# Attention values for 512 queries at once, and one MLP product moved ahead of the sums of its input

## The chip, the cores and the metric

The kernel runs on one core of a Trainium2 chip. The metric is the device time of one execution in microseconds. Engines, as the profile names them: PE is TensorE (matrix products and transposes), PEld its weight loads, DVE is VectorE, ACT is ScalarE, POOL is GpSimd, SP is SyncE, which issues DMAs.

## The reference

One layer of a hybrid block on 512 tokens of width 1024, in fp32, and a last norm:

```python
n = rmsnorm(h, g_mix)
gq, gk, gv, gr, z_gf, z_gb, cq, ckv, kr, z_ma, z_mb = split(n @ w_in)
y_gla = gla_branch(gq, gk, gv, gr, z_gf, z_gb, ...)     # 4 heads of gated linear attention
y_mla = mla_branch(cq, ckv, kr, positions, ...)         # 8 heads of softmax attention
h = h + (sigmoid(z_ma) * y_gla + sigmoid(z_mb) * y_mla) @ w_out
m = rmsnorm(h, g_mlp)
h = h + square(relu(m @ w_ff1)) @ w_ff2                 # 1024 -> 4096 -> 1024
return rmsnorm(h, g_final)

# in mla_branch, for each of 8 heads (128 value columns each):
s = einsum('bhqd,bhkd->bhqk', q, k)
p = softmax(s, axis=-1)
o = einsum('bhqk,bhkv->bhqv', p, v)
```

The change touches the last line of `mla_branch` and the order of work at the start of `m @ w_ff1`.

## The kernel before

**Precision.** A product in fp32 is done as three products of numbers split in a high and a low part (`mm3`: high by high, high by low, low by high). A split is one ACT instruction for the high part and one on DVE for the low part. Each `mm3` is thus three TensorE instructions, each with a weight load of its own.

**Order.** The body does not issue instructions at once. It records them, and `flush` gives them to a list scheduler (`Due`) with a cost for each instruction; it sets the order on each engine under the recorded dependencies, and may reorder the products on TensorE. All instructions are issued by one helper, so all of them carry line 232 in the profile, and groups are told apart by the names of tiles. PSUM has eight banks of 128x512, four with the tag `mm` and four with the tag `at`.

**Attention.** One loop over n runs over the 32 pairs of head and query tile (8 heads, 4 tiles of 128 queries). Round n normalises the pair of tiles before (in even rounds), computes scores and exponents of tile n (`s`, `top`, `e`), flips tile n - `LAG_B` (3 rounds later), and multiplies values at c = n - `LAG_C` (6 rounds later). `att_normalise` takes two tiles: one reciprocal of both sums on DVE, the first tile scaled on ACT, the second on DVE. `att_flip(head, qt)` transposes the four key tiles of one query tile into one `at` bank `tp` and splits that into `pT`, high and low, kept for a pair of query tiles (4 key tiles by 256 queries). `att_values(head, half)` multiplies one pair of query tiles: four key tiles, each one `mm3` of 128x256, so 12 TensorE instructions a half and 24 a head, into one half of the bank `av`. Halves are issued at odd c. Behind the second half `merge` multiplies by the gate on DVE (`tb<-tb,av`) and adds the other branch on POOL. The last head merges each half by itself, since the output projection waits for it. In the same rounds the next pair of heads is projected (`uq`, `uk`, `uv`), and weights of the output projection (`bo10`, `bo11`) are split.

**Output projection.** `wo_product` forms seven products (Strassen-Winograd) of 512 columns in the banks `wox`, `wow` and `woz`.

**MLP.** m is transposed row by row (`ident,ms` into `mb` banks, gained by ACT and DVE). The up projection runs in eight `Quad`s of seven products (m = 1, 5, 2, 6, 3, 7, 4), each of 24 TensorE instructions of 128x256, planned at 2.88 us. Products 1, 2 and 3 read parts of m itself; products 5, 6, 7 and 4 read sums of such parts, which `combine` and `split_m` build on DVE and ACT once all rows of m are there (`four` in the trace: `four0` and `four1` for m = 5, `four2` and `four3` for 6, `four4` and `four5` for 7). Weights of a product are staged by DMA into `wf` tiles or sums `w0s`, `w1s`, and split into one of four pairs `hl0` to `hl3`. A quad holds three banks, x, z and w, taken from the ring `mms` (banks `mb0` to `mb3`) and given back after products 2, 3 and 4; `evacuate` reads a bank into a row tile (ACT for 1, 5 and 6; DVE for 2, 3 and 7). At the start quads 0 and 1 go side by side:

```python
    quads[1].multiply(2)
    split_m(7, r01, 2)
    fm.evacuate(1, range(4, KD))
    split_m(4, r10, 3)
    groups = [Group(qd) for qd in range(NQ)]
    for m in (5, 6):
        for q in range(2):
            quads[q].multiply(m)
```

The down projection (`Group`, banks `ab` from the ring `ats` among others) follows and is interleaved with the later quads.

Of the kernel before, what the change touches and what calls it, by code (L numbers as in the profile page):

```python
# [18 lines left out]
P = 128  # L19
# [373 lines left out]
def tile_block(ctx: ExitStack, tc: tile.TileContext, t, out: bass.AP):  # L393
# [28 lines left out]
    def u4(name, dt=F32R, shape=(P, 2, S)):  # L422
        return tl(list(shape), dt, "u4", 30, name)
# [113 lines left out]
    class Flipped:  # L537
# [8 lines left out]
        def rows(self, i, xs):  # L546
            half = i // 2
            if half not in self.banks:
                self.banks[half] = [ps("at", f"{self.name}b{half}{j}") for j in range(4)]
            for k in range(KD):  # L550
                at = (k // 4) * 256 + (i % 2) * P
                nc.tensor.transpose(
                    self.banks[half][k % 4][:, at : at + P], xs[:, k * P : (k + 1) * P], ident
                )
# [901 lines left out]
        nc.vector.tensor_scalar(b, b, tot[:, 1:2], None, op0=ALU.mult)  # L1456

    def att_flip(head, qt):
        e = probs.pop((head, qt))
        if qt % 2 == 0:  # L1460
            pTs[head, qt // 2] = [u4(f"pT{head}{qt}{x}", F32R, (P, NT, 256)) for x in range(2)]
        tp = ps("at", f"tp{head}{qt}")
        for k in range(NT):
            nc.tensor.transpose(tp[:, k * P : (k + 1) * P], e[:, k * P : (k + 1) * P], ident)
        hi, lo = pTs[head, qt // 2]
        c = slice((qt % 2) * P, (qt % 2 + 1) * P)
        split(hi[:, :, c], lo[:, :, c], tp.rearrange("p (k q) -> p k q", k=NT))

    def att_values(head, half):
        if half == 0:  # L1470
            avs[head] = ps("mm", f"av{head}")
        acc = avs[head]
        hi, lo = pTs.pop((head, half))
        _, _, vs, c = heads[head]
        for k in range(NT):
            vt = vs[k // 2]
            mm3(acc[:, half * 256 : (half + 1) * 256], vt[:, 0, k % 2, c], vt[:, 1, k % 2, c],
                hi[:, k, :], lo[:, k, :], k == 0, k == NT - 1)
        if head < MH - 1:
            if half == 1:  # L1480
                merge(head, acc, (0, 1))
        else:
            merge(head, acc, (half,))

    def merge(head, acc, halves_):

        p, c = head // 2, slice((head % 2) * HT, (head % 2 + 1) * HT)
        if p not in merged:
            merged[p] = u2(f"mx{p}"), u2(f"my{p}")
        y = g2[head]  # L1490
        tok = slice(halves_[0] * HT, (halves_[-1] + 1) * HT)
        nc.vector.scalar_tensor_tensor(y[:, tok], y[:, tok], 1.0, acc[:, tok], op0=ALU.add, op1=ALU.mult)
        for x in halves_:
            t_ = slice(x * HT, (x + 1) * HT)
            nc.gpsimd.tensor_tensor(merged[p][x][:, c], y[:, t_], y1[head][:, t_], op=ALU.add)
# [151 lines left out]
    rs = gla_squares(h, os)  # L1647
    gla_gated(h, os, rs)
    LAG_B, LAG_C = 3, 6
    units = up_units(1)  # L1650
    next(units)
    sums_of, flipping, span = {}, {}, {}
    for n in range(4 * MH + LAG_C - 1):
        if n % 2 == 0 and 2 <= n <= 4 * MH:
            att_normalise((n - 2) // 4, (n - 2) % 4)
        if n < 4 * MH:
            att_scores(n // 4, n % 4)
        if 2 <= n % 8 < 7:
# [12 lines left out]
        for x, at in (("y", (18, 26, 34)), ("z", (20, 28, 36))):  # L1671
            if n in at:
                p = at.index(n)
                to = (5, 6) if x == "y" else (7, 3)
                split_sum(wo_left[p], sums_of[p, x], *to, f"{x}o{p}", nc.gpsimd if p < 2 else nc.vector)
        if n in (19, 30):
            p = (19, 30).index(n)
            split_first(wo_left[p], merged[p][0], f"o{p}", nc.gpsimd)
        if n == 35:
            split_first(wo_left[2], merged[2][0], "o2")  # L1680
        if n in (11, 13):
            streamed(1, B11, (n - 11) // 2)
            split_streamed(1, (n - 11) // 2)
        if n in (21, 23):
            streamed(2, B21, (n - 21) // 2)
        if n == 15:
            load_w2(0, B11, w_out)
        if n == 17:
            load_w2(0, B21, w_out, B22)
        if n == 23:  # L1690
            load_onto(B21, B11, w_out)
        if n == 24:
            load_w2(0, B12, w_out)
            load_w2(0, B22, w_out)
        c = n - LAG_C
        if c >= 0 and c % 2 == 1:
            att_values(c // 4, (c % 4) // 2)
        if n == 33:
            load_onto(B21, B12, w_out)
        if c > 0 and c % 8 == 7 and c // 8 < NP - 1:  # L1700
            sums_of[c // 8, "y"], sums_of[c // 8, "z"] = merged_sums(c // 8, nc.gpsimd)
# [274 lines left out]
    class Quad:  # L1976
# [5 lines left out]
        def ready(self, m):  # L1982
            self.begun[m] = self.weights(m)

        def rows(self, i, j):
            return w1_block(self.q, i, j)

# [38 lines left out]
                wfs.back(item)  # L2026
            return ready

        def multiply(self, m):
            bank = {1: "x", 5: "z", 2: "w", 6: "x", 3: "z", 7: "x", 4: "x"}[m]  # L2030
            hl, wh, wl, keys = self.weights(m)
            begin = m in (1, 5, 2)
            if begin:
                self.banks[bank] = mms.take()
            bkey, acc = self.banks[bank]
            hi, lo = m_of[m]

            def run():
                for x in range(2):
                    c = slice(x * HT, (x + 1) * HT)  # L2040
                    f = slice(x * P, (x + 1) * P)
                    for k in range(KD // 2):
                        mm3(acc[:, c], wh[:, k, f], wl[:, k, f], hi[:, k, :], lo[:, k, :],
                            begin and x == 0 and k == 0, k == KD // 2 - 1, True)

            plan.add("PE", 2.88, run, keys + m_key[m], (bkey,))
            hls.back(hl)
            self.evacuate(m, bkey, acc)
            if m in (2, 3, 4):
                mms.back(self.banks[bank])  # L2050

        def evacuate(self, m, bkey, acc):
            if m in (5, 1, 6, 4):
# [278 lines left out]
    combine(r01, r11, r01, ALU.subtract)  # L2332
    combine(r10, msum, r10, ALU.subtract)
    quads[1].multiply(2)
    split_m(7, r01, 2)
    fm.evacuate(1, range(4, KD))
    split_m(4, r10, 3)
# [7 lines left out]
    for qd, g in enumerate(groups):  # L2345
        odd = quads[2 * qd + 1]
        g.multiply(1, 0)
        if qd:
            odd.multiply(7)
        g.multiply(1, 1, (2,))  # L2350
        odd.multiply(4)
        second = 5 if g.last else 2
        g.multiply(second, 0)
        g.multiply(1, 1, (3,))
        g.multiply(second, 1)
        if g.last:
            break
        even, odd = quads[2 * qd + 2], quads[2 * qd + 3]
        for m, between in ((5, 5), (3, None), (6, 1), (7, 2), (4, None)):
            for x in range(2):  # L2360
                g.multiply(m, x)
            if between:
                even.multiply(between)
        for m in (6, 3, 7):
            even.multiply(m)
        odd.multiply(5)
        even.multiply(4)
        for m in (1, 2, 6, 3):
            odd.multiply(m)
# [46 lines left out]
```

## Time and profile before

| what | number |
| --- | --- |
| runs | 737.72, 738.91 and 3364.55 us, median 738.91 |
| the profiled execution | 737.6 us |
| its span on the core | 735.9 us |
| PE busy | 726.7 us, 99% of the span, 4214 instructions |
| DVE busy | 606.2 us, 82% |
| ACT busy | 516.7 us, 70% |
| attention's values on TensorE | 307.6 to 375.2 us of the span |
| products with m = 5 begin | 425.09 us |

A row of the waits says which engine waited for which tile of which engine, and then the microseconds in total, how often, and the longest. A piece of the chain is a start, a length and the work. In rows of the timeline the brackets name the time that the engine was idle before and what released it. "x12" is the number of instructions put together; matmuls overlap, so that the length of one is more than the time from its start to that of the next.

### The profile page before, as it was taken

Reading aid. Unit: us, or ns where it says so; the run is one execution under the profiler, and the core shown is the slowest. Engines: PE = TensorE matmul, PEld = TensorE weight load, DVE = VectorE, ACT = ScalarE, POOL = GpSimd, SP = SyncE. Lnnn points to the kernel's source line nnn. Section 1 sums busy time; section 2 is a strip of 40 time slices with the busy share of each in tenths; the row PEclk is TensorE's granted clock in tenths of the full one; section 3 lists DMA queues with packets and bytes.
Section 4 is the critical chain, followed back from the end, with each engine's and each line's share of the span. In section 5 each row is a group of like instructions: output and inputs, shape, how many; then the busy total and the mean of one; then the engine's idle time right before and its main releaser. Section 6 shows DMA issues by size and latency. Waiting matters only on the chain.

```text
span 735.9 us, 11540 instructions
## 1 busy us (share of the span) xinstructions
PE 726.7 (99%) x4214; PEld 640.5 (87%) x4214; DVE 606.2 (82%) x959; ACT 516.7 (70%) x863; POOL 201.6 (27%) x208
## 2 busy tenths in 40 slices
PE   8999999999999999999999999999999999999996
PEld 7888888888898888899988999889988998889985
DVE  6694776759999769998988899878985798778885
ACT  7574666659999657989955798647864587448744
POOL 1133031301111215038753421321132212212433
PEclk9999999999999999999999999999999999999999
DMA  9969896652312223339996899998899997988993
GB/s 312 331 142 166 215 201 113 115 115 57 87 49 68 32 53 94 72 86 256 245 289 109 178 204 251 164 243 185 207 205 207 214 209 178 216 223 194 191 167 115
DMA packets 105050, 124.39 MB, mean 169 GB/s; under 512 B 16176, under 2 KB 68416, under 8 KB 104992
## 3 DMA queue, kind: packets, MB, share of 16 engines
q0 software_dynamic: 33024, 51.14, 41.9%
q1 hardware_dynamic: 71680, 71.97, 32.1%
q8 instruction: 33, 0.54, 0.3%
q10 hardware_dynamic: 288, 0.52, 0.2%
q14 instruction: 25, 0.20, 0.1%
HBM read 119.95 MB, written 2.10 MB: 166 GB/s over the span
## 4 chain that ended last, share of the span: by engine, by line
PE 93%; DVE 3%; ACT 2%; issue 1%; DMA 1%; POOL 1%; POOLq 0%; DVEq 0%; ACTq 0%
PE mb L232 25%; PE ab L232 16%; PE zb L232 4%; PE av L232 3%; PE s L232 3%; PE wox L232 3%; PE gvx L232 3%; PE zax L232 3%; PE grx L232 3%; PE first L232 3%; PE cq L232 2%; PE tp L232 2%; PE uv L232 2%; PE gvz L232 2%; PE ckv L232 1%; PE gq L232 1%
## 5 line engine op out<-in xcount | busy, mean ns | idle before, releaser
L232 POOL DMA_DIRECT2D ms<-in_w_ff x37 | 47.5, 1365 | 116.7 <-DVE hl3l L232 28.4
L232 POOL DMA_DIRECT2D w1s<-in_w_ff x19 | 24.1, 1269 | 75.4 <-DVE hl0l L232 25.2
L232 DVE TENSOR_TENSOR h<-h,ab 128x512 f32<-128x512 f32 x48 | 31.7, 682 | 8.2 <-PE ab L232 8.2
L232 ACT ACTIVATE row<-row 128x512 f32<-128x512 f32 x56 | 35.1, 627 | 1.1 <-DVE row L232 0.3
L232 PE MATMUL s<-kbuf,q 96*128 96x512 f32 x96 | 28.2, 407 | 0.0
L232 PE MATMUL av<-pT,v 128*128 128x256 f32 x192 | 27.5, 288 | 0.0
L232 PE MATMUL mb<-four,hl3h 128*128 128x256 f32 x144 | 26.6, 283 | 0.0
L232 PEld LDWEIGHTS av<-pT,v 128*128 128x128 f32 x192 | 24.6, 190 | 0.3
L232 PE MATMUL mb<-four,hl0h 128*128 128x256 f32 x128 | 24.0, 284 | 0.7 <-ACT row L232 0.5
L232 ACT ACTIVATE e<-s,top 128x512 f32<-128x512 f32 x32 | 22.1, 695 | 3.4 <-DVE top L232 3.1
L232 DVE TENSOR_REDUCE top<-s 128x1 f32<-128x512 f32 x32 | 21.5, 685 | 3.5 <-PE s L232 3.3
L232 ACT ACTIVATE row<-mb 128x512 f32<-128x512 f32 x32 | 18.7, 586 | 7.8 <-PE mb L232 7.6
L232 PE MATMUL mb<-four,hl1h 128*128 128x256 f32 x128 | 23.5, 283 | 0.0
L232 PEld LDWEIGHTS mb<-four,hl3h 128*128 128x128 f32 x144 | 22.8, 191 | 0.5
L232 DVE TENSOR_TENSOR pT<-tp,pT 128x512 fp32r<-128x512 f32 x32 | 21.4, 680 | 1.2 <-ACT pT L232 1.2
L232 ACT ACTIVATE hl2h<-ms 128x1024 fp32r<-128x1024 f32 x13 | 13.8, 1059 | 11.9 <-PE ab L232 6.1
L232 PEld LDWEIGHTS mb<-four,hl0h 128*128 128x128 f32 x128 | 20.3, 191 | 1.3 <-ACT row L232 0.7
L232 ACT ACTIVATE hl0h<-ms 128x1024 fp32r<-128x1024 f32 x11 | 11.6, 1058 | 12.9 <-PE ab L232 8.7
L232 PE MATMUL mb<-four,hl2h 128*128 128x256 f32 x112 | 20.6, 283 | 0.0
L232 PE MATMUL mb<-m,hl1h 128*128 128x256 f32 x112 | 20.6, 283 | 0.0
L232 PEld LDWEIGHTS mb<-four,hl1h 128*128 128x128 f32 x128 | 20.2, 192 | 0.2
L232 PE MATMUL mb<-four,hl3l 128*128 128x256 f32 x72 | 20.3, 283 | 0.0
(1101 smaller groups left out, 2781.5 us busy)
## 6 DMA issues: line engine op xcount, KB each, us to landing
ms<-in_w_ff POOLq DMA_DIRECT2D x37, 512.0 KB, 7.5
w1s<-in_w_ff POOLq DMA_DIRECT2D x19, 512.0 KB, 7.4
ms<-in_w_ff SPq DMA_DIRECT2D x16, 512.0 KB, 5.6
w1s<-in_w_ff SPq DMA_DIRECT2D x15, 512.0 KB, 5.8
wf0f<-in_w_ff SPq DMA_DIRECT2D x11, 512.0 KB, 5.8
wf1f<-in_w_ff SPq DMA_DIRECT2D x11, 512.0 KB, 6.3
wf2f<-in_w_ff SPq DMA_DIRECT2D x11, 512.0 KB, 7.1
w<-in_w_out POOLq DMA_DIRECT2D x10, 512.0 KB, 7.7
```

The lines of the kernel that those rows point to most:

```text
L232: return call(*map(real, work.args), **{k: real(v) for k, v in work.named.items()})
```

## The change

Two things are changed.

For heads 0 to 6 (head 7 keeps the old body of `att_flip`, left out in the diff below), a flip no longer turns the four key tiles of one query tile, but two key tiles of two query tiles (`pair` counts the query pairs, `kp` the key pairs). `pT` then holds two key tiles by all 512 queries, and a half of the values is a pair of key tiles instead of a pair of query tiles: two `mm3` of 128x512 that write the whole bank. A head has 12 TensorE instructions for its values, with 512 columns each. They are issued at c % 4 = 2 and 3 (`AV_AT`). Head 7 is as before. Transposes and splits are as many and as large as before.

In the MLP the first product of quad 2 (it reads m itself) is put in behind `quads[1].multiply(2)`, ahead of the sums, and its bank is left unread (`hold`) until the place in the first group's loop where that product stood. Quads 0 and 1 take their bank z from the ring `ats`.

```diff
     def att_flip(head, qt):
-        e = probs.pop((head, qt))
-        if qt % 2 == 0:
-            pTs[head, qt // 2] = [u4(f"pT{head}{qt}{x}", F32R, (P, NT, 256)) for x in range(2)]
+        if head == MH - 1:
...
+            return
+        pair, kp = qt // 2, qt % 2
+        if pair == 0:
+            pTs[head, kp] = [u4(f"pT{head}{qt}{x}", F32R, (P, 2, S)) for x in range(2)]
         tp = ps("at", f"tp{head}{qt}")
-        for k in range(NT):
-            nc.tensor.transpose(tp[:, k * P : (k + 1) * P], e[:, k * P : (k + 1) * P], ident)
-        hi, lo = pTs[head, qt // 2]
-        c = slice((qt % 2) * P, (qt % 2 + 1) * P)
-        split(hi[:, :, c], lo[:, :, c], tp.rearrange("p (k q) -> p k q", k=NT))
+        for k in range(2):
+            for t_ in range(2):
+                e = probs[head, 2 * pair + t_]
+                at = (2 * kp + k) * P
+                nc.tensor.transpose(tp[:, (2 * k + t_) * P : (2 * k + t_ + 1) * P], e[:, at : at + P], ident)
+        hi, lo = pTs[head, kp]
+        c = slice(pair * 256, (pair + 1) * 256)
+        split(hi[:, :, c], lo[:, :, c], tp.rearrange("p (k q) -> p k q", k=2))

     def att_values(head, half):
+        if head < MH - 1:
+            if half == 0:
+                avs[head] = ps("mm", f"av{head}")
+            acc = avs[head]
+            hi, lo = pTs.pop((head, half))
+            _, _, vs, c = heads[head]
+            for k in range(2):
+                vt = vs[half]
+                mm3(acc, vt[:, 0, k, c], vt[:, 1, k, c], hi[:, k, :], lo[:, k, :], half == k == 0, half == k == 1)
+            if half == 1:
+                merge(head, acc, (0, 1))
+            return
...
     LAG_B, LAG_C = 3, 6
+    AV_AT = ((2, 3), (1, 3))
...
-        if c >= 0 and c % 2 == 1:
-            att_values(c // 4, (c % 4) // 2)
+        if c >= 0 and c % 4 in AV_AT[c // 4 == MH - 1]:
+            att_values(c // 4, AV_AT[c // 4 == MH - 1].index(c % 4))
...
+        def ring(self, bank):
+            return ats if self.q < 2 and bank == "z" else mms
...
-        def multiply(self, m):
+        def multiply(self, m, hold=False):
...
-                self.banks[bank] = mms.take()
+                self.banks[bank] = self.ring(bank).take()
...
             hls.back(hl)
+            if hold:
+                return
             self.evacuate(m, bkey, acc)
             if m in (2, 3, 4):
-                mms.back(self.banks[bank])
+                self.ring(bank).back(self.banks[bank])
...
     quads[1].multiply(2)
+    quads[2].multiply(1, True)
     split_m(7, r01, 2)
...
-            if between:
+            if between == 1 and qd == 0:
+                even.evacuate(1, *even.banks["x"])
+            elif between:
                 even.multiply(between)
```

What the scheduler makes of it is seen at three places. The first is TensorE at the first values (`tp` are flips, named by head and query tile; `s` scores; `av` values; `uq` a projection for the next heads). Before:

```order
L232 MATMUL tp02_626_3131<-ident_63,e02_598_3045 128x128 x4
L232 MATMUL s12_627_3139<-kbuf1_538_2867,q01_566_2843 128x512 x3
L232 MATMUL s13_640_3146<-kbuf1_538_2867,q01_566_2843 128x512
L232 MATMUL tp03_639_3149<-ident_63,e03_603_3074 128x128 x4
L232 MATMUL s13_640_3146<-kbuf1_538_2867,q01_566_2843 128x512 x2
L232 MATMUL tp10_645_3162<-ident_63,e10_614_3108 128x128 x4
L232 MATMUL av0_646_3170<-pT000_605_3082,v00_572_2911 128x256
L232 MATMUL av0_646_3170<-pT001_606_3104,v00_572_2911 128x256
```

and with the change:

```order
L232 MATMUL tp02_626_3132<-ident_63,e02_598_3045 128x128
L232 MATMUL tp02_626_3132<-ident_63,e03_603_3074 128x128
...
L232 MATMUL tp03_639_3152<-ident_63,e02_598_3045 128x128
L232 MATMUL tp03_639_3152<-ident_63,e03_603_3074 128x128
...
L232 MATMUL av0_653_3161<-pT000_605_3082,v00_572_2911 128x512
L232 MATMUL uq2_664_3166<-cqhl0_533_2722,wq2h_632_2931 128x512
L232 MATMUL tp10_645_3169<-ident_63,e10_614_3117 128x128
L232 MATMUL av0_653_3161<-pT001_606_3106,v00_572_2911 128x512
...
L232 MATMUL tp10_645_3169<-ident_63,e11_623_3134 128x128
```

The third flip, `tp02`, now reads `e02` and `e03`; the first product of the values has 512 columns, and the values of head 0 are spread among flips and scores instead of standing together.

On DVE the same stretch, where `e03` is normalised (`tot` the sums, `top` the largest score, `pT` the low parts). Before:

```order
L232 TENSOR_REDUCE top_613_3095<-s10_612_3064 128x1
L232 TENSOR_TENSOR pT001_606_3104<-tp00_607_3041,pT000_605_3082 128x4x128
L232 RECIPROCAL tot_599_3044<-tot_599_3044 128x2
L232 TENSOR_REDUCE top_620_3115<-s11_619_3102 128x1
L232 TENSOR_SCALAR e03_603_3074<-e03_603_3074,tot_599_3044 128x512
L232 TENSOR_SCALAR v10_617_3100<-uv10_616_3072,v10_617_3100 128x512
L232 TENSOR_TENSOR pT001_606_3104<-tp01_618_3093,pT000_605_3082 128x4x128
```

and with the change:

```order
L232 TENSOR_REDUCE top_613_3095<-s10_612_3064 128x1
L232 RECIPROCAL tot_599_3044<-tot_599_3044 128x2
L232 TENSOR_TENSOR pT001_606_3106<-tp00_607_3041,pT000_605_3082 128x2x256
L232 TENSOR_SCALAR e03_603_3074<-e03_603_3074,tot_599_3044 128x512
L232 TENSOR_REDUCE top_622_3121<-s11_621_3102 128x1
L232 TENSOR_SCALAR v10_617_3100<-uv10_616_3072,v10_617_3100 128x512
L232 TENSOR_TENSOR pT011_619_3139<-tp01_620_3093,pT010_618_3126 128x2x256
```

The reciprocal moves ahead of a `pT`, and the normalising of `e03` ahead of a reduction `top`.

The third place is TensorE at the start of the MLP's sums (`mb3<-m10` is quad 1's product 2; `four0`, `four1` belong to product 5, `four4` to product 7). Before, the end of product 2 and the place where quad 0's product 7 begins:

```order
L232 MATMUL mb3_929_4593<-m100_911_4433,hl3h_924_4510 128x256
L232 MATMUL mb3_929_4593<-m101_912_4456,hl3h_924_4510 128x256
L232 MATMUL mb3_929_4593<-m100_911_4433,hl3l_925_4551 128x256
L232 MATMUL mb1_927_4507<-four0_960_4630,hl0h_918_4395 128x256
L232 MATMUL mb1_927_4507<-four1_961_4639,hl0h_918_4395 128x256
...
L232 MATMUL mb2_928_4545<-four2_962_4672,hl3h_924_4510 128x256
L232 MATMUL mb2_928_4545<-four3_963_4699,hl3h_924_4510 128x256
L232 MATMUL mb0_926_4437<-four4_964_4696,hl0h_918_4395 128x256
L232 MATMUL mb2_928_4545<-four2_962_4672,hl3l_925_4551 128x256
```

and with the change:

```order
L232 MATMUL mb3_929_4508<-m101_912_4359,hl3h_924_4420 128x256
L232 MATMUL mb3_929_4508<-m100_911_4329,hl3l_925_4441 128x256
L232 MATMUL mb1_927_4381<-m000_909_4354,hl0h_918_4321 128x256
L232 MATMUL mb1_927_4381<-m001_910_4377,hl0h_918_4321 128x256
...
L232 MATMUL ab0_930_4592<-four0_960_4561,hl1h_920_4335 128x256
L232 MATMUL ab0_930_4592<-four1_961_4576,hl1h_920_4335 128x256
...
L232 MATMUL mb2_928_4458<-four3_963_4650,hl0h_918_4321 128x256
L232 MATMUL mb2_928_4458<-four2_962_4628,hl0l_919_4332 128x256
L232 MATMUL mb0_926_4393<-four4_964_4643,hl1h_920_4335 128x256
L232 MATMUL mb0_926_4393<-four5_965_4666,hl1h_920_4335 128x256
```

Between `mb3<-m10` and the first product that reads `four0` stand now the 24 instructions of `mb1<-m00`, quad 2's first product; `mb1` was quad 0's product 5 before, which now goes to `ab0`. Quad 0's product 7 (`mb0<-four4`), which stood two instructions into quad 1's product 6 (`mb2`), now follows the whole of it.

More of the change, by code (lines that the diff above doesn't have):

```diff
@@ L1458, in att_flip @@
     def att_flip(head, qt):
-        e = probs.pop((head, qt))
-        if qt % 2 == 0:
-            pTs[head, qt // 2] = [u4(f"pT{head}{qt}{x}", F32R, (P, NT, 256)) for x in range(2)]
-        tp = ps("at", f"tp{head}{qt}")
-        for k in range(NT):
-            nc.tensor.transpose(tp[:, k * P : (k + 1) * P], e[:, k * P : (k + 1) * P], ident)
-        hi, lo = pTs[head, qt // 2]
-        c = slice((qt % 2) * P, (qt % 2 + 1) * P)
-        split(hi[:, :, c], lo[:, :, c], tp.rearrange("p (k q) -> p k q", k=NT))
-    def att_values(head, half):
+        if head == MH - 1:
+            e = probs.pop((head, qt))
+            if qt % 2 == 0:
+                pTs[head, qt // 2] = [u4(f"pT{head}{qt}{x}", F32R, (P, NT, 256)) for x in range(2)]
+            tp = ps("at", f"tp{head}{qt}")
+            for k in range(NT):
+                nc.tensor.transpose(tp[:, k * P : (k + 1) * P], e[:, k * P : (k + 1) * P], ident)
+            hi, lo = pTs[head, qt // 2]
+            c = slice((qt % 2) * P, (qt % 2 + 1) * P)
+            split(hi[:, :, c], lo[:, :, c], tp.rearrange("p (k q) -> p k q", k=NT))
+            return
+        pair, kp = qt // 2, qt % 2
+        if pair == 0:
+            pTs[head, kp] = [u4(f"pT{head}{qt}{x}", F32R, (P, 2, S)) for x in range(2)]
+        tp = ps("at", f"tp{head}{qt}")
+        for k in range(2):
[6 more added lines that the diff above has]
+        split(hi[:, :, c], lo[:, :, c], tp.rearrange("p (k q) -> p k q", k=2))
+    def att_values(head, half):
+        if head < MH - 1:
[10 more added lines that the diff above has]
+            return
         if half == 0:
@@ L1478, in att_values @@
                 hi[:, k, :], lo[:, k, :], k == 0, k == NT - 1)
[L1479 to L1483, printed above, removed]
+        merge(head, acc, (half,))
     def merge(head, acc, halves_):
```

## The prediction

> **What bounds the kernel now.** I read the engine totals and the slices first, then TensorE's waits, then the chain that ended last, and only then the two stages that the change touches.
>
> ```profile
> span 735.9 us, 11540 instructions
> PE 726.7 (99%) x4214; PEld 640.5 (87%) x4214; DVE 606.2 (82%) x959; ACT 516.7 (70%) x863; POOL 201.6 (27%) x208
> PE   8999999999999999999999999999999999999996
> DVE  6694776759999769998988899878985798778885
> PEclk9999999999999999999999999999999999999999
> PE 93%; DVE 3%; ACT 2%; issue 1%; DMA 1%; POOL 1%; POOLq 0%; DVEq 0%; ACTq 0%
> ```
>
> TensorE is busy in every slice but the first and the last, at a clock that was never held back, and it makes up 93% of the chain. So two things alone can shorten the middle of the program: fewer or shorter TensorE instructions, and the few moments in which TensorE stands. Those moments are these, all of them:
>
> ```profile
> PE warm L232 <- DVE ones L232: 1.1, 1, 1.1
> PE first L232 <- ACT xT L232: 0.5, 1, 0.5
> PE mb L232 <- ACT row L232: 0.5, 1, 0.5
> PE mb L232 <- DVE four L232: 0.2, 1, 0.2
> PE first L232 <- DVE first0l L232: 0.2, 1, 0.2
> ```
>
> Three belong to the start. The two of `mb` belong to the MLP's beginning, and the change works on them. In attention there is no wait at all, though DVE and ACT are hardly ever free there (columns: PE, weight loads, DVE, ACT, POOL busy us with counts, clock, DMA share, GB/s; the sum is over 298 to 380 us):
>
> ```profile
> 298.00:310.00 12.00, 12.00 (x86) 10.81 (x85) 11.05 (x22) 11.84 (x27) 0.00 (x0) 1.00 0.29 73
> 350.00:360.00 10.00, 10.00 (x74) 9.13 (x72) 9.41 (x19) 9.13 (x22) 7.37 (x10) 1.00 1.08 276
> sum 82.00, PE 82.00 PEld 74.23 DVE 75.36 ACT 71.61 POOL 43.24; mean PE 10.25 PEld 9.28 DVE 9.42 ACT 8.95 POOL 5.41
> ```
>
> DVE is idle for 82.0 - 75.4 = 6.6 us of these 82, some 0.8 us a head. TensorE leads here by a small margin, and what the change does to DVE's order is where it can go wrong.
>
> **Part 1: values in 512 columns.** Of 192 products of 128x256, the 24 of the last head stay; 168 become 84 of 128x512. Columns multiplied are as many as before, so only what a product costs beside its columns can go. The durations in the group rows overlap (288 ns each), so I take the time from start to start, from pieces of the chain that run without a break:
>
> ```profile
> L232 PE MATMUL av<-pT,v 128*128 128x256 f32 x192 | 27.5, 288 | 0.0
> 307.85 1.44 PE av L232 x12
> 311.55 1.43 PE av L232 x12
> 377.55 5.44 PE wow L232 x24
> 382.99 5.44 PE woz L232 x24
> L232 PE MATMUL wow<-bo20h,gao 128*128 128x512 f32 x8 | 2.6, 389 | 0.0
> ```
>
> Twelve products of 256 columns take 1.43 to 1.44 us, 0.120 each. Twenty-four of 512 columns take 5.44 us (from 377.55 to 382.99), 0.227 each. A head costs 24 x 0.1196 = 2.87 us before and 12 x 0.2267 = 2.72 us after: 0.15 us a head, **1.0 us** for seven. With the ends of the rounding (1.43 and 1.44 for twelve) it is 7 x 0.14 = 0.98 to 7 x 0.16 = 1.12 us. All of it is on TensorE's path. The weight loads fall by 84 too; they run under the products (PEld 640.5 us beside PE's 726.7), and I give nothing for them.
>
> [...]
>
> **Part 2: flips over two query tiles.** The number of transposes, of banks and of elements split is the same; what changes is when they may begin. A bank now holds two key tiles of two query tiles, so its second transpose needs the second tile's `e`, which DVE normalises; before, the first flip of a pair needed ACT's tile only. The rows around the third flip of head 0:
>
> ```profile
> 303.74 0.16 DVE L232 RECIPROCAL tot<-tot 128x2 f32<-128x2 f32 x1
> 303.81 0.67 DVE L232 TENSOR_REDUCE top<-s 128x1 f32<-128x512 f32 x1
> 304.40 0.48 DVE L232 TENSOR_SCALAR e<-e,tot 128x512 f32<-128x512 f32 x1
> 304.94 0.60 PE L232 MATMUL tp<-ident,e 128*128 128x128 f32 x4
> L232 PE MATMUL av<-pT,v x192: 277/283/365, 307.6 to 375.2; 128*128 128x256 f32 x192
> L232 ACT ACTIVATE e<-s,top 128x512 f32<-128x512 f32 x32 | 22.1, 695 | 3.4 <-DVE top L232 3.1
> ```
>
> DVE ends the second tile at 304.88, and TensorE flips the third tile at 304.94: 0.06 us apart, which did not matter before. In the change's order this flip stands at the same place on TensorE and needs that tile; the normalising comes one reduction (0.6 us) earlier on DVE, so here it passes. From there on the second tile of a pair has two rounds from its scores to its flip where it had three. The values run over 30 rounds in 375.2 - 307.6 = 67.6 us, 2.25 us a round; a tile's own work (reduction 0.67, exponent 0.70, reciprocal 0.16, normalising 0.48) is 2.0 of the two rounds' 4.5 when each step finds its engine free. The rest goes to queues. By hand through the order at the third flip of head 1, where a split of `bo10` (1.2 us) stands ahead of the normalising on DVE, I find less than a microsecond to spare. Behind a flip that waits stand the next scores on TensorE, and these feed the next reduction on DVE. Bounds: nothing, where the spare microsecond holds, as it holds in every round of before; and half a microsecond a head (one normalising, 0.48), 3.5 us for seven, where it holds nowhere. Rows are nearest to the first, since TensorE has other products to run ahead of a flip, and these 82 us of before show no wait; I take **+0.4 us**, one wait for all heads.
>
> **Part 3: quad 2's first product ahead.** Here are the two waits, and what feeds the first:
>
> ```profile
> 425.09 0.28 PE L232 MATMUL mb<-four,hl0h 128*128 128x256 f32 x1
> 425.57 0.38 PE L232 MATMUL mb<-four,hl0h 128*128 128x256 f32 x1 [0.20 <-DVE four L232]
> 425.79 0.28 PE L232 MATMUL mb<-four,hl0l 128*128 128x256 f32 x1
> 434.17 0.40 PE L232 MATMUL mb<-four,hl3h 128*128 128x256 f32 x2
> 435.02 0.39 PE L232 MATMUL mb<-four,hl0h 128*128 128x256 f32 x1 [0.45 <-ACT row L232]
> 435.25 0.28 PE L232 MATMUL mb<-four,hl3l 128*128 128x256 f32 x1
> 421.71 1.03 PE L232 MATMUL mb<-ident,ms 128*128 128x128 f32 x8
> 409.96 0.37 SPq L232 DMA_DIRECT2D wf1f<-in_w_ff  x1
> 418.83 1.22 DVE L232 TENSOR_TENSOR hl1l<-w1s,hl1h 128x1024 fp32r<-128x1024 f32 x1
> 423.43 1.42 DVE L232 TENSOR_TENSOR ms<-ms,ms 128x512 f32<-128x512 f32 x2 [2.38 <-ACT ms L232]
> 424.82 0.69 DVE L232 TENSOR_TENSOR four<-ms,four 128x512 fp32r<-128x512 f32 x1
> 426.03 0.68 DVE L232 TENSOR_TENSOR four<-ms,four 128x512 fp32r<-128x512 f32 x1
> 425.00:430.00 5.00, 4.80 (x41) 4.60 (x40) 5.00 (x7) 4.78 (x10) 0.00 (x0) 1.00 0.64 108
> ```
>
> The first wait: the second product starts 0.48 us behind the first instead of 0.12, and the one behind it comes after 0.22 instead of 0.12: 0.36 + 0.10 = 0.46 us. The second: two products from 434.17 would let the next start at 434.41; it starts at 435.02, and the following one 0.11 late: 0.61 + 0.11 = 0.72 us. Together **1.18 us**, which is all that part 3 can bring, since the product itself (24 x 0.12 = 2.87 us) is only moved from further back.
>
> Does it pass? Quad 2's weights need a split on DVE of 1.22 us, which the new order puts ahead of the scaling of row 3; its like is the split at 418.83. So the transposes at 421.71, ACT's gains and the sum at 424.82 come up to 1.2 us later, and `four` is there near 425.5 + 1.2 = 426.7. TensorE, with 2.87 us put in ahead, asks for it at 425.1 + 2.9 = 428.0. The first wait goes with 1.2 us to spare. The second was quad 0's seventh product, two products into quad 1's sixth, for a bank that ACT had yet to read; in the new order all 24 products of quad 1's sixth stand between, 2.87 us against the 0.45 waited. So it goes as well. But the sums behind (m = 6, 7, 4) each begin up to 1.2 us later with 2.9 us more cover, and the splits of two further weights come between them; I keep 0.3 us for a new wait there. The bounds are -1.18 and, if one split of 1.22 us falls in front of a sum that TensorE already waits for with no cover left, +0.5 (1.2 less the 0.72 of the wait that is surely gone). I take **-0.9 us**.
>
> The bank of quads 0 and 1 that moves to the other ring costs no instruction; that ring of four is free once attention and its flips are over. DMAs: the moved weight's tile is issued at 409.96 in before, as soon as its buffer is free, so no transfer is later. The tail stands as it was.
>
> **Sum.** The profiled execution took 737.6 us (span 735.9 and 1.7 around it); the median of the runs shown is 738.9, with 737.7 as the lowest, so the profiled one is a good run and 0.2% lies between good ones. 737.6 - 1.0 + 0.4 - 0.9 = **736.1 us**.
>
> **Rivals.** (A) *Only the values count.* The first MLP wait comes back as a wait of like size at m = 6 or 7, since the sums on DVE and ACT are as long as before and two more splits stand among them. For it: DVE works without a break from 425 to 430. Against it: 2.87 us of cover. 737.6 - 1.0 + 0.4 = 737.0.
>
> (B) *The flips wait for DVE* (slower). Each flip of a pair stands behind DVE's normalising; with 0.8 us idle a head DVE cannot run ahead, and each of seven heads loses one normalising, 0.48 us, and more where a reduction of 0.67 stands in front. For it: 0.06 us at the third flip, 93% busy DVE. Against it: no wait in before, and products to run in between. 737.6 - 1.0 - 0.9 + 7 x 0.5 = 739.2; it ends above before as soon as a head loses more than 1.9 / 7 = 0.27 us.
>
> (C) *Wider products bring next to nothing*, because what a 256-column product takes beyond its columns comes back with the wider reads of `pT`. For it: only the products `wow` and `woz` stand for 512 columns here, and they read other tiles. Against it: two tiles alike at 0.227. [...]
>
> **How the numbers follow.** The forecast 0.5, A 0.17, B 0.25, C 0.08. Own range of the forecast: -1.12 - 1.18 gives 735.3, and with 0.7 us of scatter (half of the 738.9 - 737.6 between good runs) 734.6 below. Above, B's 739.2 and a little of the same scatter: 739.6. A difference of 2%, 14.8 us, is about what a measurement of this kernel can tell from no change, and no case here comes near it: even with a wait of 0.48 at every one of the 28 flips, 13.4 us, and nothing gained, it stays below. Faster by over 2%: 0.01; within: 0.96; slower: 0.03.
>
> **What would show it.** Twelve `av` products of 512 columns in 2.72 us a head where they run unbroken; no entry `PE tp <- DVE e` in TensorE's waits; the two `mb` entries gone, none of more than 0.3 us in their place; busy time of PE down by about 1.0. A wait of `tp` for `e` would mean B; a wait of `mb` for `four` near 428 to 440 would mean A; a head at 2.85 us would mean C. A time above 739.6 with none of these would make the whole reading wrong.

## The result, and the profile after

The change takes 736.47 us (median), before 737.63 us in the same series of runs: a ratio of 0.9983, 95% interval 0.9977 to 0.9988. By the ratio that is 1.25 us less (0.9 to 1.7), by the two medians 1.16. The kernel is faster, by less than the 2% named in the prediction. The profiled execution took 736.4 us, with this page:

```profile
span 734.7 us, 11376 instructions
PE 725.5 (99%) x4130; PEld 634.9 (86%) x4130; DVE 605.0 (82%) x959; ACT 515.9 (70%) x863; POOL 201.8 (27%) x208
PE 96%; ACT 1%; POOL 1%; issue 1%; DMA 1%; DVE 0%; POOLq 0%; DVEq 0%; ACTq 0%
```

TensorE is still what ends the program. TensorE's list of waits is now this, whole:

```profile
PE first L232 <- ACT xT L232: 1.2, 1, 1.2
PE warm L232 <- DVE ones L232: 1.1, 1, 1.1
PE first L232 <- DVE first0l L232: 0.2, 1, 0.2
```

Both entries of `mb` are gone, and none of `tp` or `av` has come. (The 1.2 us of the first line stand in the start, where TensorE runs through stand-in products until x is there; the first work behind it begins at 6.43 us, at 6.56 before.) To see where the 1.2 us of the span went, I take fixed points on TensorE from the timeline: the first product of the scores and the first of `woz`. Before:

```profile
293.20 1.77 PE L232 MATMUL s<-kbuf,q 96*128 96x512 f32 x7
382.83 0.39 PE L232 MATMUL woz<-bo50h,ghyo 128*128 128x512 f32 x1
```

and with the change:

```profile
293.06 1.77 PE L232 MATMUL s<-kbuf,q 96*128 96x512 f32 x7
382.34 0.39 PE L232 MATMUL woz<-bo50h,ghyo 128*128 128x512 f32 x1
```

Up to the scores 0.14 us went, all of it in the program's start, which the change doesn't touch. Attention took 89.63 us and now takes 89.28: **0.35 us** less. From `woz` to TensorE's last product 346.50 became 345.81 us: **0.69 us** less. The tail is the same. So behind the start two thirds of the gain came in the stage that holds the MLP, and attention gained a third of what its products promised.

**The values.** Their groups in the change (the form of 512 columns, then that of the last head), and pieces of its chain, with those of `uk` and `wow` for comparison:

```profile
L232 PE MATMUL av<-pT,v 128*128 128x512 f32 x84 | 24.7, 410 | 0.0
L232 PE MATMUL av<-pT,v 128*128 128x256 f32 x24 | 3.4, 285 | 0.0
311.20 1.40 PE av L232 x6
325.08 1.39 PE av L232 x6
316.73 1.37 PE uk L232 x6
378.43 4.08 PE wow L232 x18
```

Six products of 512 columns take 1.39 to 1.40 us, 0.232 each; eighteen of `wow` take 4.08, 0.227 each. A run of values is short, six at the most, and stays above the 0.227 us on which the prediction was built. In experiment 6 below, where the same values stand in runs of up to twelve, four of the five runs of eleven or twelve come down to 0.227 from their fourth to eighth product on (its run of eleven at 360.56 us takes 2.52, 0.229 each), so it is not the wider read of `pT`. Shortness alone is not the reason either, since `uk` has runs of six at 0.228 here; what keeps the first products of a run near 0.232 isn't shown.

Counted over the stage, TensorE's products and flips stand in 125 runs of one kind of tile where there were 102, and the 128 transposes in 39 groups instead of 32. I add up the whole stage from start to start, and put the 0.08 to 0.09 us by which a product comes late behind a group of flips down to the flips. Then the values take 22.3 us instead of 23.0, **0.7 us** less, and everything else (flips, scores, projections, `wox`) takes **0.4 us** more for the same number of instructions.

**The MLP's start.** TensorE where product 5 begins, and in quad 1's product 6; then what the latter waits for:

```profile
427.57 0.28 PE L232 MATMUL mb<-m,hl0l 128*128 128x256 f32 x1
427.69 0.40 PE L232 MATMUL ab<-four,hl1h 128*128 128x256 f32 x2
427.93 0.28 PE L232 MATMUL ab<-four,hl1l 128*128 128x256 f32 x1
436.33 0.40 PE L232 MATMUL mb<-four,hl0h 128*128 128x256 f32 x2
436.85 0.39 PE L232 MATMUL mb<-four,hl0l 128*128 128x256 f32 x1
435.57 1.23 DVE L232 TENSOR_TENSOR hl0l<-w1s,hl0h 128x1024 fp32r<-128x1024 f32 x1 [0.33 <-ACT hl0h L232]
433.53 1.06 ACT L232 ACTIVATE hl2h<-w1s 128x1024 fp32r<-128x1024 f32 x1 [0.80 <-PE ab L232]
434.50 1.04 ACT L232 ACTIVATE hl0h<-w1s 128x1024 fp32r<-128x1024 f32 x1
```

Into product 5 TensorE goes without a stop (427.69 is 0.12 behind 427.57). In quad 1's product 6 the third instruction starts 0.52 us behind the first where 0.24 is usual, and the one behind it another 0.10 late: 0.38 us, too short to stand in the list of waits. The low part `hl0l` is late because ACT's high part of it stood behind that of another weight, which itself waited 0.80 us.

### The profile page after: what moved, and what is told of

Same layout as the page of the kernel before. It is cut to its first block, busy times and chain, and to the rows that moved or that the text cites. A ratio compares the mean times of both kernels' runs of the same rounds, so it can differ in the third digit from the quotient of the medians.

```text
span 734.7 us, 11376 instructions
## 1 busy us (share of the span) xinstructions
PE 725.5 (99%) x4130; PEld 634.9 (86%) x4130; DVE 605.0 (82%) x959; ACT 515.9 (70%) x863; POOL 201.8 (27%) x208
## 4 chain that ended last, share of the span: by engine, by line
PE 96%; ACT 1%; POOL 1%; issue 1%; DMA 1%; DVE 0%; POOLq 0%; DVEq 0%; ACTq 0%
PE mb L232 24%; PE ab L232 18%; PE zb L232 4%; PE s L232 3%; PE av L232 3%; PE wox L232 3%; PE gvx L232 3%; PE zax L232 3%; PE grx L232 3%; PE first L232 3%; PE cq L232 2%; PE gq L232 2%; PE gk L232 2%; PE tp L232 2%; PE uv L232 2%; PE gvz L232 2%
## 5 line engine op out<-in xcount | busy, mean ns | idle before, releaser
L232 PE MATMUL av<-pT,v 128*128 128x512 f32 (+1 forms) x108 | 28.1, 382 | 0.0
L232 PE MATMUL mb<-four,hl3h 128*128 128x256 f32 x128 | 23.4, 283 | 0.0
L232 ACT ACTIVATE pT<-tp 128x512 fp32r<-128x512 f32 x32 | 19.1, 597 | 3.0 <-PE tp L232 2.4
L232 PE MATMUL mb<-four,hl0l 128*128 128x256 f32 x72 | 20.5, 284 | 0.1
L232 PEld LDWEIGHTS mb<-four,hl3h 128*128 128x128 f32 x128 | 20.2, 192 | 0.3
L232 PE MATMUL tp<-ident,e 128*128 128x128 f32 x128 | 20.3, 272 | 0.0
L232 PEld LDWEIGHTS av<-pT,v 128*128 128x128 f32 x108 | 17.8, 189 | 2.6
L232 PEld LDWEIGHTS s<-kbuf,q 96*128 96x128 f32 x96 | 16.6, 189 | 3.3 <-ACT e L232 0.5
L232 PEld LDWEIGHTS tp<-ident,e 128*128 128x128 f32 x128 | 15.9, 140 | 3.9 <-ACT pT L232 0.3
L232 POOL DMA_DIRECT2D zaw<-in_w_in x8 | 9.5, 1190 | 33.6 <-DVE za50l L232 18.8
```

The source lines that it names most:

```text
L232: return call(*map(real, work.args), **{k: real(v) for k, v in work.named.items()})
```

## The experiments

Each kernel ran in five rounds beside the kernel before; ratios are to that. "Attention" is the time from the first score to the first `woz` as above (89.63 before, 89.28 with the change), "rest" that from there to TensorE's last product (346.50 and 345.81), both from the profiled execution.

| kernel | ratio, 95% interval | median us | attention | rest |
| --- | --- | --- | --- | --- |
| the change | 0.9983 (0.9977 to 0.9988) | 736.47 | 89.28 | 345.81 |
| values only | 1.0018 (1.0009 to 1.0027) | 738.84 | 89.29 | 347.68 |
| MLP part only | 0.9991 (0.9982 to 1.0000) | 737.13 | 89.63 | 345.89 |
| ring only | 1.0003 (0.9995 to 1.0012) | 738.05 | 89.61 | 346.75 |
| change, values in 256 columns | 0.9996 (0.9988 to 1.0005) | 737.75 | 90.33 | 345.43 |
| change without the product ahead | 1.0044 (1.0032 to 1.0056) | 740.87 | 89.21 | 350.09 |
| change, `av` kept together | 1.0062 (1.0047 to 1.0077) | 741.24 | 91.92 | 346.70 |
| the same, both halves at 3 | 1.0049 (1.0037 to 1.0061) | 741.25 | 92.81 | 347.18 |
| change, two splits swapped | 0.9988 (0.9980 to 0.9997) | 736.74 | 89.25 | 346.14 |
| change, ring for quad 1 only | 0.9988 (0.9979 to 0.9997) | 736.63 | 89.25 | 346.11 |
| change, first half at 1 | 1.0010 (1.0001 to 1.0019) | 738.38 | 89.23 | 347.62 |
| values only, roots first | 1.0033 (1.0021 to 1.0045) | 740.23 | 89.27 | 349.77 |
| without the product, roots first | 1.0072 (1.0059 to 1.0086) | 743.20 | 89.23 | 353.30 |

**1. Values only.**

```diff
-            return ats if self.q < 2 and bank == "z" else mms
+            return mms
...
     quads[1].multiply(2)
-    quads[2].multiply(1, True)
...
```

with the first group's loop as before.

> Only the attention part of the change; the MLP's start is as before. Stage lengths are taken from TensorE's start stamps: from the first product of the scores to the first of woz, 89.63 us before and 89.29 with the change. Theory 1 (the two parts add up and hardly meet): 89.3 us in this stage again, both MLP waits of before (0.46 and 0.72 us) back, time 0.3 to 0.4 us below before. Theory 2 (the values bring the whole 1.0 us and the MLP part hides a loss): 1.0 us below before.

Attention came out as with the change, 89.29 us, but the kernel is slower than before, by 0.18%. Neither theory had that. TensorE's list of waits has, besides the start:

```profile
PE mb L232 <- DVE four L232: 0.8, 1, 0.8
PE mb L232 <- ACT four L232: 0.6, 1, 0.6
```

and the timeline where product 5 begins:

```profile
424.80 0.28 PE L232 MATMUL mb<-m,hl3l 128*128 128x256 f32 x1
425.65 0.38 PE L232 MATMUL mb<-four,hl0h 128*128 128x256 f32 x1 [0.57 <-ACT four L232]
425.87 0.38 PE L232 MATMUL mb<-four,hl1h 128*128 128x256 f32 x1
427.06 0.39 PE L232 MATMUL mb<-four,hl0h 128*128 128x256 f32 x1 [0.82 <-DVE four L232]
```

Two stops of 0.73 and 1.07 us beyond the usual 0.12, and 0.5 of restarts and a third stop behind them: 2.3 us, where before had 1.18. TensorE was 0.34 us earlier at `woz` and 0.17 us earlier here (424.80, before 424.97), and the sums came later than before. So the two parts don't add up: alone, the values lose.

**2. The MLP part only.**

```diff
-    AV_AT = ((2, 3), (1, 3))
+    AV_AT = ((1, 3), (1, 3))
```

with `att_flip` and `att_values` as they were before.

> Only the MLP part (product ahead and bank z from the other ring); attention as before. Theory 1: attention's stage at 89.6 us, the waits of 1.18 us gone and a wait of some 0.4 us for a weight's low part in quad 1's product 6 in their place, 0.7 us below before. Theory 2: nothing below 0.3 us, since sums and splits only move.

Theory 1 came true: attention 89.63, the rest 0.61 us shorter, one wait of `mb` for `hl0l` (0.3 in the list) in place of the two. The time is 0.09% below before; its interval reaches to no difference, and the profiled execution lost 0.6 us in an earlier stage that this edit leaves alone (a wait of `y` for `gra`).

**3. The ring only.**

```diff
     quads[1].multiply(2)
-    quads[2].multiply(1, True)
```

(of experiment 2, with the first group's loop as before).

> Of the MLP part only the ring: bank z of quads 0 and 1 from the other four banks; no product is put ahead. In the order quad 0's product 7 then already stands behind all 24 products of quad 1's product 6. Theory 1 (the ring alone takes the second wait away, the product ahead only the first): the wait of 0.72 us at product 7 is gone, the one of 0.46 us at product 5 stays, time 0.7 us below before, the same as with the product put ahead. Theory 2 (the product ahead is what gives cover): both waits stay, time as before.

Half of theory 1 holds: the wait at product 7 went. But the one at product 5 grew from 0.46 to 1.5 us:

```profile
424.92 0.28 PE L232 MATMUL mb<-m,hl3l 128*128 128x256 f32 x1
426.42 0.51 PE L232 MATMUL ab<-four,hl0h 128*128 128x256 f32 x2 [1.22 <-ACT ms L232]
```

The ring alone gains nothing measurable (0.9995 to 1.0012).

**4. The values in 256 columns.**

```diff
-                mm3(acc, vt[:, 0, k, c], vt[:, 1, k, c], hi[:, k, :], lo[:, k, :], half == k == 0, half == k == 1)
+                for x in range(2):
+                    q = slice(x * 256, (x + 1) * 256)
+                    mm3(acc[:, q], vt[:, 0, k, c], vt[:, 1, k, c], hi[:, k, q], lo[:, k, q], half == k == 0, half == k == 1, True)
```

What this kernel returns is off by 0.11 (relative error), for a reason that no run shows; it stands here for its times alone. Nor is all else quite the same: the scheduler makes 136 runs of one kind of tile of it, where the change has 125.

> The whole change, but each value product of 512 columns is issued as two of 256 columns (same flips of two tiles, same places); 168 products of 256 columns again. Theory 1 (a 512-column product costs 0.231 us in runs as short as here, not 0.227): attention's stage grows over the 89.29 us of the change by 84 x (0.240 - 0.231) = 0.7 us, to 90.0. Theory 2 (width brings the full 1.0 us and flips of two tiles cost 0.7): it grows by 1.0 to 1.1 us, to 90.3 or more, with waits of tp for e.

Attention took 90.33 us, 1.05 above the change and 0.70 above before. By the number theory 2 is nearer, but its waits are not there: no `tp` waits for `e`. What the stage has are four stops of 0.10 to 0.14 us, 0.45 together, too short for the list, where the change has one of 0.10. Here is one, four products of 256 columns that take 0.62 us from their start to the transpose instead of 0.48:

```profile
350.38 0.64 PE L232 MATMUL av<-pT,v 128*128 128x256 f32 x4
351.00 0.30 PE L232 MATMUL tp<-ident,e 128*128 128x128 f32 x1
```

Without them the width is worth 1.05 - 0.35 = 0.7 us, near theory 1's price, which by the rows above is 84 x (2 x 0.1196 - 0.232) = 0.6. The run doesn't part the two sharply, since the order moved with the width.

**5. The change without the product ahead.**

```diff
     quads[1].multiply(2)
-    quads[2].multiply(1, True)
...
```

> The whole change but for the product put ahead: values of 512 columns and bank z from the other ring, quad 2's first product where it was. Theory 1 (each part alone only makes TensorE arrive earlier at a chain on ACT and DVE, and only the product put ahead covers that chain): attention's stage 89.3 us, a wait of 1.5 to 2 us ahead of product 5, time 0.3 to 1.2 us above before. Theory 2 (values and ring add up, the product brings nothing): 0.5 us or more below before.

Slower than before by 0.44%, in the direction of theory 1 and far beyond its size; it is 4.4 us slower than the change. TensorE waits 3 us ahead of product 5, and behind the wait its clock is down:

```profile
428.05 0.50 PE L232 MATMUL ab<-four,hl0h 128*128 128x256 f32 x2 [2.89 <-ACT ms L232]
428.00:432.00 4.00, 3.95 (x20) 3.96 (x21) 4.00 (x7) 3.04 (x7) 1.29 (x1) 0.57 0.26 37
```

In the four microseconds behind the wait the granted clock is 0.57 and 20 instructions start, where 33 of 0.12 us would have. This run shows what the product ahead is worth: with values and ring in place, it covers a chain on ACT and DVE that otherwise costs 3 us of waiting and 1.5 of slow clock.

**6 and 7. Values kept together.** The scheduler's choice on TensorE prefers products of the `av` bank that it has begun; in 7 both halves are issued at c % 4 = 3.

```diff
...
+                    run = lambda i: not (todo[i].outs[0][0] is on and on.name.startswith(('av',)))
-                    i = min((i for i in among if ready[i] <= t + 0.02), key=lambda i: (late[i], i))
+                    i = min((i for i in among if ready[i] <= t + 0.02), key=lambda i: (run(i), late[i], i))
...
```

> The whole change, and the scheduler goes on with products of av once it has begun some, as long as they are ready. TensorE changes from one kind of tile to another 110 times in attention's stage instead of 125. Theory 1 (the missing 0.7 us of the values lies in these changes, 0.03 us each): the stage falls from 89.29 to 88.8 us, and the time by 0.4 us. Theory 2 (it lies in what DVE and ACT do meanwhile): 89.3 us.

> As the run before, and both halves of a head are issued at c % 4 = 3; 105 changes of tile. Theory 1: the stage falls to 88.7 us, 0.6 below the change; time about 736.0. Theory 2: 89.3 us. If flips or scores then wait for DVE, waits of tp or s appear in TensorE's list.

Both theories failed: attention grew to 91.92 and 92.81 us. Of the waits, the first below stands in both, the second in experiment 7 alone; the third row is a run of eleven values in the chain of experiment 6:

```profile
PE av L232 <- ACT pT L232: 0.7, 1, 0.7
PE tp L232 <- DVE e L232: 0.6, 1, 0.6
360.56 2.52 PE av L232 x11
```

Values that stand together ask for their splits sooner than ACT and DVE have them: TensorE waits 0.7 us for `pT`, and in experiment 7 its flips 0.6 us for `e`. The values' being spread among flips and scores, which leaves them in short runs, is here also what keeps TensorE busy (89.28 us, against 91.92 and 92.81 with the values together). In experiment 7 the clock fell to 0.50 from 358 to 360 us of the span, behind several stops from 354 on. Whether the changes of tile themselves cost anything stays open, since there are no runs here with fewer of them and no waits.

**8. Two splits swapped.** `highs` lists the high parts in the order in which they are recorded.

```diff
...
+    sixth = highs[-1]
     for q, m in ((0, 7), (1, 7), (0, 3), (0, 4), (1, 3)):
         quads[q].multiply(m)
+        if m == 7 and q == 1:
+            highs[-1].behind.append(sixth)
```

> The whole change, with the split of the weight of quad 1's product 7 on ACT put behind that of its product 6, which stood behind it while it waited 0.8 us for a product. Theory 1 (the last MLP wait, 0.28 us and 0.10 behind it, comes from this order on ACT alone): it goes, time 0.4 us below the change. Theory 2 (the sum of that weight lands too late anyway): the wait stays.

Theory 1's wait went, its gain didn't come: the wait for `hl0l` is gone, and the list of waits has another in its place, `mb` for a `row` of ACT (0.5): quad 0's product 7 moved back to two instructions into quad 1's product 6. The time is that of the change within the intervals.

**9. The ring for quad 1 only.**

```diff
-            return ats if self.q < 2 and bank == "z" else mms
+            return ats if self.q == 1 and bank == "z" else mms
```

> The whole change, but only quad 1 takes bank z from the other ring; quad 0 takes it from mms as before. In the order quad 0's product 7 then stands two products into quad 1's product 6 again. Theory 1 (the ring serves the second wait, the product ahead the first): no wait ahead of product 5, a wait on a row of ACT of about 0.5 to 0.7 us at product 7, time 0.2 to 0.5 us above the change, as there the 0.38 us at product 6 goes and this comes. Theory 2 (with the product put ahead the ring does not matter): the list of waits as with the change, same time.

As theory 1 said: no stop at product 5, and at product 7

```profile
437.09 0.50 PE L232 MATMUL mb<-four,hl1h 128*128 128x256 f32 x2 [0.45 <-ACT row L232]
```

By its ratio it can't be told from the change, though its rest is 0.30 us longer in the profile: the ring for quad 0 trades a stop of 0.7 us for one of 0.38. The product ahead without any bank from the other ring was not run.

**10. The first half one round earlier.**

```diff
-    AV_AT = ((2, 3), (1, 3))
+    AV_AT = ((1, 3), (1, 3))
```

> The whole change, but the first half of a head's values is issued at c % 4 = 1 as before, one round earlier than in the change and two rounds behind the flip that it needs instead of three. Theory 1 (what counts is that flips have their splits done when the values ask): the scheduler spreads the values, 126 changes of tile, and small waits of av for pT appear; attention's stage 0.3 to 1 us longer than 89.29. Theory 2 (three rounds are not needed): 89.3 us and the time of the change.

In attention theory 2 holds: 89.23 us. Yet the kernel is 1.9 us slower than the change, since at the MLP's start product 5 waits again, in spite of the product ahead, and a second wait follows at 485 us:

```profile
427.24 0.28 PE L232 MATMUL mb<-m,hl0l 128*128 128x256 f32 x1
428.33 0.50 PE L232 MATMUL ab<-four,hl1h 128*128 128x256 f32 x2 [0.81 <-ACT ms L232]
```

An edit in attention that leaves attention as long as it was moves the MLP's start by more than attention ever gained.

**11 and 12. Roots first.** In experiments 1 and 5 the scheduler put the issue of a transfer (it adds onto `w0s`) ahead of the two inverse roots of rows 2 and 3 on POOL:

```profile
414.87 1.27 POOL L232 DMA_DIRECT2D w0s<-in_w_ff  x1 [3.14 <-DVE hl0l L232]
415.65 2.60 POOL L232 TENSOR_TENSOR hp<-hp,mhalf 128x1 f32<-128x1 f32 x2
418.38 0.71 ACT L232 ACTIVATE ms<-h,hp 128x512 f32<-128x512 f32 x1
```

These are rows of experiment 1. Before, the first root began at 413.40 and row 2 was scaled at 416.99. The edit puts the transfer behind both roots (`pows` lists the roots, `behind` what has to stand ahead of an instruction):

```diff
...
                 add = load_add(a, self.rows(0, 0), self.ka)
+                if self.q == 0:
+                    add.behind.extend(pows[-2:])
```

> Only the values (as in the first run of this study), with one order forced on POOL: the issue of the transfer that adds onto w0s stands behind the two inverse roots of rows 2 and 3, where the scheduler had put it ahead of both (before: between the two). Theory 1 (the values alone lost time because that issue holds the roots, and with them the scaling of rows 2 and 3 and product 5, back by 1.4 us): row 2 is scaled on ACT near 417 instead of 418.4, the waits ahead of product 5 fall from 2.2 us to 1.2 to 1.5, time 0.7 us or more below the first run, at or below before. Theory 2 (the chain is late for other reasons): waits of 2 us again, time as in the first run.

> As the run without the product ahead (values and ring), with the same order forced on POOL. Theory 1: the wait of 3.05 us ahead of product 5 falls by 1 us or more, the clock stays at 1.0 behind it, and the time falls by 2 us or more from 740.9. Theory 2: as in that run.

The first step of theory 1 held and its sum did not. In experiment 11 row 2 is scaled at 411.47, and the stops of product 5 fell from 2.3 to 0.95 us. But the transfer is now issued at 420.48 instead of 414.87, and `hl2h`, split from `w0s`, is begun on ACT at 431.68 instead of 425.50. TensorE waits there for `hl3h` and `hl2h`, and the longest wait, for a sum of the down projection at 459 us, is new too:

```profile
PE ab L232 <- ACT four L232: 1.1, 1, 1.1
PE mb L232 <- ACT hl3h L232: 0.5, 1, 0.5
PE mb L232 <- ACT hl2h L232: 0.4, 1, 0.4
420.48 1.81 POOL L232 DMA_DIRECT2D w0s<-in_w_ff  x1
```

In experiment 12 the wait ahead of product 5 fell from 3.05 to 1.98 us and the clock stayed up behind it, as theory 1 had it. Then the same two weights are late, and a sum is waited for at 460 us:

```profile
PE ab L232 <- ACT four L232: 1.9, 1, 1.9
PE ab L232 <- ACT ms L232: 1.8, 1, 1.8
```

Both kernels are slower than those without the forced order. POOL's queue here carries the roots that TensorE's next input needs and the transfers that its later weights need; the order between them only chooses which comes late.

## Why the prediction came out right, point by point

- **The sum.** Forecast 1.5 us below the profiled execution of before (736.1 against 737.6); measured 1.25 us below by the ratio and 1.2 in the profiles. The time lies in the forecast's range, and the rivals A (737.0) and B (739.2) lie outside the interval of the ratio (735.9 to 736.7 on 737.63). Part of the closeness is luck: the two stages gave 0.35 and 0.69 us where the terms had 0.6 (1.0 less 0.4) and 0.9, and the 0.14 us from the program's start belongs to no term.
- **Part 1, mis-sized.** 1.0 us was the term; attention gave 0.35. The step that failed is the price of a 512-column product, taken from 24 of `wow` in a row. In runs of six they cost 0.232, which makes the term 84 x (0.2392 - 0.232) = 0.6 us; counted over the whole stage the values saved 0.7. That is 2.78 us for a head, halfway between the 2.72 that the prediction named for itself and the 2.85 that it named for C. No run shows the 2.85, nor that a wider product brings next to nothing: the values saved 0.7. Part 1 has no term for the neighbours of the values, and these took 0.4 us more. More groups of transposes and changes of tile came with the new flips, but that these are the cause is not shown: experiments 6 and 7, meant to take them away, brought waits instead.
- **Part 2, right in sign, for another reason.** I put in 0.4 us for one wait of a flip for DVE. There is no such wait. That the neighbours of the values took about as much more is luck. The mechanism exists: once the values stand together (experiment 7), `tp` waits 0.6 us for `e`.
- **Part 3, right.** 1.18 us less 0.3 for a new wait was forecast, 0.69 came: both waits went, and the new one is the 0.38 us at `hl0l`; these make 0.80, and why the stage shows 0.11 less isn't traced. The cover was forecast with 1.2 us to spare, and TensorE did go straight into product 5. But what takes which wait away I told only for the change as a whole. Experiments 1, 3, 5 and 9 show that the product ahead carries nearly all: without it the values and the ring each make product 5 wait longer (2.3 and 1.5 us, both together 3), and with it the ring for quad 0 makes no difference that the times show.
- **What no rival had:** that the parts are not independent. I added them as if the MLP's start saw only when TensorE arrives. The scheduler orders all engines again with each edit, and the rows' scaling on POOL, ACT and DVE moves by one to two microseconds with it. The first part alone is slower than before.

## What to carry to other kernels

TensorE was busy for 99% of the span here, and the values alone brought it 0.17 us earlier to product 5 and made the kernel 0.18% slower. Where one engine is as busy, look first at the next chain of the other engines that it arrives at, and put work of its own in front of that chain before saving elsewhere: the product put ahead kept 4.4 us here. A price for an instruction is taken from runs like those that it will stand in (0.232 us in runs of six, 0.227 in one of eighteen). With a scheduler, an edit is not confined to the place where it is made: compare the stages one by one, and not only the total.

## What the runs showed of the hardware that was not expected

- TensorE's granted clock fell to half behind some stops, each time for 3.41 us: 428.43 to 431.84 in experiment 5, 357.58 to 361.00 in experiment 7, 463.16 to 466.57 in experiment 12. A stop's length alone didn't decide: in experiment 12 one of 2.0 us at 460 us was followed by half clock, and one of 2.0 us at 424 us was not. The rows below are stretches of 3.41 us, the length of such a fall, the first two of experiment 7, the others of experiment 12, whose time is divided at 463.16, where the clock fell (columns as in the prediction):

```profile
354.17:357.58 3.41, 1.94 (x9) 1.13 (x8) 3.41 (x6) 1.94 (x5) 3.41 (x5) 1.00 1.11 262
357.58:361.00 3.42, 3.42 (x11) 2.83 (x10) 3.42 (x5) 2.23 (x5) 3.42 (x5) 0.50 1.07 339
422.20:425.61 3.41, 2.29 (x20) 2.08 (x18) 2.30 (x4) 3.28 (x8) 0.00 (x0) 1.00 1.12 168
425.61:429.02 3.41, 2.71 (x22) 2.71 (x23) 3.34 (x7) 3.18 (x8) 0.00 (x0) 1.00 0.82 127
459.74:463.16 3.42, 1.56 (x7) 0.97 (x6) 2.96 (x8) 3.42 (x7) 0.00 (x0) 1.00 0.94 239
463.16:466.57 3.41, 3.41 (x10) 2.63 (x9) 3.26 (x5) 2.70 (x5) 1.18 (x1) 0.50 0.04 12
```

The stop at 424 us falls on two stretches, with TensorE busy for 2.29 and 2.71 us; the one at 460 us falls into one, with 1.56. In experiment 7 the fall stands behind several short stops in one stretch (1.94 us busy), so TensorE had worked for up to 1.94 us in the stretches ahead of a fall. Busy time alone didn't decide either: in experiment 9 the stretch from 726.55 to 729.96 us, with 1.83 us busy in 16 products, left the clock at 1.00, where the 1.94 us of experiment 7 are 9 instructions. What does decide isn't shown.
- A product of 512 columns cost 0.232 us in the values' runs of six and 0.227 in a run of eighteen, one of 256 columns 0.120. Put in place of two products of 256 columns (0.239), the wide one gained 0.012 us at the price of the long run and 0.007 at that of the short ones.
